# Decoder trunk on one core: every second half unit of up's weights gets its low part from an accumulating transfer, and the front end is written in another order

## The chip, the cores and the metric

The kernel runs on one core of a Trainium2 chip. Its engines run side by side, each through its own list of instructions in order: PE (matrix products), ACT (scalar engine), DVE (vector engine), POOL (GpSimd) and SP (here a queue that issues transfers); ACT and POOL issue transfers too. The metric is the device time of one execution in microseconds (us), as the median of several runs.

## What is computed

Two layers, then a final norm, on 256 tokens of width 1024. Cut to what matters here:

```python
for l in range(2):
    h = rmsnorm(x, g_mix[l])
    proj = h @ w_in[l]                      # 1024 x 8192: q, k, v, gates of two kinds of attention
    ...                                     # retention and stick-breaking attention
    x = x + merged @ w_out[l]
    h = rmsnorm(x, g_mlp[l])
    up = square(relu(h @ w_up[l]))          # w_up: 1024 x 4096
    x = x + up @ w_down[l]                  # w_down: 4096 x 1024
return rmsnorm(x, g_final)
```

All of it is float32. A product is made of three matrix products in a reduced format (fp32r): each operand is split into a high part (the rounded value) and a low part (the value minus the high part), and high x high, high x low and low x high are added.

## The kernel before

**The weights as a stream.** All weight matrices are cut into units of 512 rows x 512 columns (1 MB), listed in the order of use; class WeightStream walks the list. `load` brings a unit into one of 3 raw tiles [128, 4, 512] (SP queue). `_split` works on a half unit [128, 2, 512]: ACT copies it into an fp32r tile `whi` (L73, the high part), DVE subtracts (L78) and writes `wlo` (the low part). There are 4 buffers of `whi` and 4 of `wlo`. `take` hands the next half to the matrix products and first calls `ahead`, which writes the splits up to 3 halves ahead (LOOKAHEAD) and the loads up to 2 units ahead (RAW_AHEAD). So the split of a half starts when PE is through with the half four places earlier, and a unit's load starts when the raw tile three units earlier has been read.

**The products.** `cols512` runs 4 halves into a set of PSUM banks. `half_T` (L281, L283, L285) serves the first projections, `half_W` (L299 with `whi`, L301 with `wlo`) serves k and up, `half_N` (L319 to L321) the rest. For each of the four groups g of the MLP there are 4 units of up (two calls of `cols512`: banks `pa`, then `pb`) and 4 units of down. After each call of up, `evac_up` joins the bank halves (`joined`: ACT copy L308, DVE add L309), takes relu (ACT L721) and square (ACT L722) and splits the result (ACT L180, DVE L181). This evacuation runs beside the next call's halves.

**The front end.** x is brought in four pieces of 256 columns on ACT's queue, the first unit in four pieces and the second in two on SP's queue, then the third unit and the constants `cst`, `tab`, `dec`. PE turns x (`turned`, L204), ACT and DVE apply the gain column and split (`gain_split`, L194 and L195). The gain columns `gcol` of both norms come from one small transposition of `gn` (L174).

**What sets the order.** The kernel is written with tiles; a scheduler puts each engine's instructions in an order at build time and inserts the waits. Some instructions of the front end are pinned to the written order. A wait in a list below such as DMASW1 is for a transfer issued from POOL, DMAHW1 for one issued from SP or ACT, PE_, DVE_ and Activation_ for those engines; the number behind a tile's name tells tiles of one name apart.

Of the kernel before, what the change touches and what calls it, by code (L numbers as in the profile page):

```python
# [10 lines left out]
F32 = mybir.dt.float32  # L11
F32R = mybir.dt.float32r
BF16 = mybir.dt.bfloat16
AF = mybir.ActivationFunctionType
ALU = mybir.AluOpType
PSUM = bass.MemoryType.PSUM

P = 128
# [22 lines left out]
class WeightStream:  # L41

    def __init__(self, nc, pools, units):
        self.nc = nc
        self.raw_pool, self.hi_pool, self.lo_pool = pools
        self.units = units
        self.raw = []
        self.parts = {}  # L50
        self.split = 0
        self.pos = 0
        self.between = self.pin = None

    def load(self, pieces=1, between=lambda j: None):
        u = len(self.raw)
        t = self.raw_pool.tile([P, 4, 512], F32, tag="raw", name=f"raw{u}")
        src = self.units[u].rearrange("(k p) n -> p k n", p=P)
        n = 4 // pieces
        for j in range(pieces):  # L60
            self.nc.sync.dma_start(out=t[:, j * n:(j + 1) * n, :], in_=src[:, j * n:(j + 1) * n, :])
            between(j)
        self.raw.append(t)

    def _split(self, h):
        src = self.raw[h // 2][:, 2 * (h % 2):2 * (h % 2) + 2, :]
        hi = self.hi_pool.tile([P, 2, 512], F32R, tag="hi", name=f"whi{h}")
        lo = self.lo_pool.tile([P, 2, 512], F32R, tag="lo", name=f"wlo{h}")
        for i, sl in enumerate((slice(0, 1), slice(1, 2)) if h < 2 else (slice(0, 2),)):
            if h == 0 and i == 0:  # L70
                self.nc.vector.tensor_copy(out=hi[:, sl], in_=src[:, sl])
            else:
                m = self.nc.scalar.copy(out=hi[:, sl], in_=src[:, sl])  # L73
                if h < 3:
                    self.pin(m)
            if h == 0:
                self.between(i)
            m = self.nc.vector.tensor_tensor(out=lo[:, sl], in0=src[:, sl], in1=hi[:, sl].bitcast(F32),  # L78
                                             op=ALU.subtract)
            if h < 3:  # L80
                self.pin(m)
        self.parts[h] = (hi, lo)
# [16 lines left out]
def kernel(ctx, tc, x, w_in, p_ret, p_sb, w_out, w_up, w_down, g_mix, g_mlp, g_final,  # L99
                      c_sq, c_tab, c_decay, out):  # L100
    nc = tc.nc
    const = ctx.enter_context(tc.tile_pool(name="const", bufs=1))
    big = ctx.enter_context(tc.tile_pool(name="big", bufs=1))
    raw_pool = ctx.enter_context(tc.tile_pool(name="raw", bufs=3))
    hi_pool = ctx.enter_context(tc.tile_pool(name="hi", bufs=4))
    lo_pool = ctx.enter_context(tc.tile_pool(name="lo", bufs=4))
    wk = ctx.enter_context(tc.tile_pool(name="wk", bufs=2))
    small = ctx.enter_context(tc.tile_pool(name="small", bufs=2))
    psA = ctx.enter_context(tc.tile_pool(name="psA", bufs=4, space=PSUM))
    psB = ctx.enter_context(tc.tile_pool(name="psB", bufs=4, space=PSUM))  # L110


    units = []

    def add(w, r0, c0):
        units.append(w[r0:r0 + 512, c0:c0 + 512])

    def add_cols(w, c0, n):
        for c in range(c0, c0 + n, 512):
            add(w, 0, c)  # L120
            add(w, 512, c)

    for l in range(DEPTH):
        for n, wd in (("q_s", 1024), ("k_s", 1024), ("v_s", 1024), ("q_r", 512), ("k_r", 512),
                      ("v_r", 1024), ("g_r", 1024), ("g_a", 1024), ("g_b", 1024)):
            add_cols(w_in[l], OFF[n], wd)
        for c in (0, 512):
            for w in (p_sb[l], p_ret[l]):
                add(w, 0, c)
                add(w, 512, c)  # L130
        add_cols(w_out[l], 0, D)
        for g in range(4):
            add_cols(w_up[l], g * 1024, 1024)
            for c in (0, 512):
                add(w_down[l], g * 1024, c)
                add(w_down[l], g * 1024 + 512, c)


    xs = big.tile([P, 2, D], F32, tag="x", name="x")
    xv = x[0].rearrange("(t p) d -> p t d", p=P)  # L140
    ident = const.tile([P, P], F32, name="ident")
    gn = const.tile([32, P], F32, name="gn")
    ws = WeightStream(nc, (raw_pool, hi_pool, lo_pool), units)
    tc.keep_in_program_order(nc.scalar.preload_act_table_set("natural_log_exp_and_others"))
    nc.scalar.dma_start(out=ident, in_=c_sq[:, 0, :])
    nc.sync.dma_start(out=gn[0:16, :], in_=g_mix.rearrange("l (k p) -> (l k) p", p=P))
    nc.sync.dma_start(out=gn[16:32, :], in_=g_mlp.rearrange("l (k p) -> (l k) p", p=P))
    for j in range(4):
        c = slice(j * 256, (j + 1) * 256)
        nc.scalar.dma_start(out=xs[:, :, c], in_=xv[:, :, c])  # L150
    ws.load(4)
    ws.load(2)
    ws.load()
    cst = const.tile([P, 2, P], F32, name="cst")
    nc.sync.dma_start(out=cst, in_=c_sq[:, 1:3, :])
    tri_f, ones = cst[:, 0, :], cst[:, 1, :]
    tab = const.tile([P, 2, S], F32, name="tab")
    nc.sync.dma_start(out=tab, in_=c_tab)
    dec = const.tile([P, RH + 1, S], F32, name="dec")
    nc.sync.dma_start(out=dec, in_=c_decay)  # L160


    warm = wk.tile([P, 512], F32, tag="t2", name="warm").bitcast(BF16)[:, 0:512]
# [3 lines left out]
    def busy(n):  # L167
        for _ in range(n):
            tc.keep_in_program_order(nc.tensor.matmul(wps, lhsT=warm[:, 0:P], rhs=warm, start=True, stop=True))

    busy(WARM)

    gps = psA.tile([P, 512], F32, tag="a", name="gps")
    nc.tensor.transpose(gps[:, :32], gn, ident[0:32, 0:32])  # L174
    gcol = const.tile([P, 32], F32, name="gcol")
    nc.scalar.copy(out=gcol, in_=gps[:, :32])
    busy(2)

    def split_to(hi, lo, src):
# [37 lines left out]
    def rstd_rows(r):  # L217

        dg = wk.tile([P, 2, S], F32, tag="t1", name="dg")[:, 0, :]
        for t in range(2):  # L220
            nc.vector.tensor_scalar(dg[:, t * P:(t + 1) * P], ident, r[:, t:t + 1], None, ALU.mult)
        bc = psB.tile([P, 512], F32, tag="b", name="bc")
        nc.tensor.matmul(bc[:, :S], lhsT=ones, rhs=dg, start=True, stop=True)
        rb = wk.tile([P, S], F32, tag="rb", name="rb", bufs=1)
        nc.vector.tensor_copy(out=rb, in_=bc[:, :S])
        return rb

    class Norm:


        def __init__(self, gi):
            self.gi = gi
            self.ms = small.tile([P, 4], F32, tag="ms4", name="ms4")
            self.h = paired("h", "h")
# [109 lines left out]
    between = []  # L344
# [13 lines left out]
    def paired(tag, name):  # L358

        return [big.tile([P, 2, 2, S], F32R, tag=f"{tag}{i}", name=name) for i in range(4)]  # L360
# [13 lines left out]
    onesr = const.tile([P, P], F32R, name="onesr")  # L374

    def mix(l, norm):
        h = norm.h
        state = {"n": 0}


        def norm_tick():
            state["n"] += 1
            if l == 0 and state["n"] <= 4:
                tc.keep_in_program_order(norm.square(*divmod(state["n"] - 1, 2)))
            if state["n"] == 4:
                state["rc"] = norm.rstd()
                if l == 0:
                    tc.keep_in_program_order(nc.vector.tensor_copy(out=trir, in_=tri_f))
                    nc.vector.tensor_copy(out=onesr, in_=ones)
            if state["n"] == 5:  # L390
                rc = state["rc"]
                rb = rstd_rows(rc)
                rcs = small.tile([P, 2], F32, tag="rcs", name="rcs")
                nc.vector.tensor_scalar(rcs, rc[:, 0:2], P ** -0.5, None, ALU.mult)
                cr = wk.tile([P, S], F32, tag="cr", name="cr", bufs=1)
                sr = wk.tile([P, S], F32, tag="sr", name="sr", bufs=1)
                nc.vector.tensor_tensor(out=cr, in0=tab[:, 0, :], in1=rb, op=ALU.mult)
                nc.vector.tensor_tensor(out=sr, in0=tab[:, 1, :], in1=rb, op=ALU.mult)
                state.update(rb=rb, rcs=rcs, cr=cr, sr=sr)
            if state["n"] == 6:  # L400
                state["evac"]()

        qs = paired("q", "qs")
        q1 = big.tile([P, SH, P], F32, tag="qb", name="q1")
# [14 lines left out]
        def put_v(hi, lo, src, t):  # L419
            nc.scalar.activation(hi, src, AF.Identity, scale=rc[:, t:t + 1])  # L420
            nc.vector.scalar_tensor_tensor(out=lo, in0=src, scalar=rc[:, t:t + 1], in1=hi.bitcast(F32),
                                           op0=ALU.mult, op1=ALU.subtract)

        banks0 = cols512(half_T, h, norm_tick)
        state["evac"] = lambda: evac_q(0, banks0)
        evac_q(1, cols512(half_T, h, norm_tick))
        rc, rb, rcs = state["rc"], state["rb"], state["rcs"]
        for c in range(2):
# [312 lines left out]
    for l in range(DEPTH):  # L741
        norm = mlp(l, mix(l, norm))
# [46 lines left out]
```

## Time and profile before

| | us |
|---|---|
| median of 3 runs (914.57 to 915.81) | 914.61 |
| the profiled execution's own time | 914.65 |
| its span, first to last instruction | 912.9 |
| PE busy | 903.2 (99%) |
| DVE busy | 609.6 (67%) |
| ACT busy | 523.2 (57%) |
| POOL busy, 18 instructions | 9.6 (1%) |

The busy share is an average over the whole span. Which engine holds the others is read from the waits: who stood idle, until what, and for how long, in the stretch that is spoken of. The chain of work that ended last, followed back from the end, lies on PE for 97% of the span.

### The profile page before, as it was taken

How to read it: one execution, taken by the hardware profiler on the slowest of the kernel's cores; microseconds unless marked ns; L12 is line 12 of the kernel's file. 1: busy time of each engine (PE TensorE's matmuls, PEld its weight loads, DVE VectorE, ACT ScalarE, POOL GpSimd, SP SyncE). 2: the span in 40 equal slices, each digit the busy share in tenths (PEclk: the TensorE clock that was granted, in tenths of full speed). 3: DMA queues.
4: the chain of work that ended last, by engine and by line, in shares of the span. 5: the costliest groups of instructions: out<-in, count | busy, mean ns of one | idle time of the engine just before them, and what ended most of it. 6: DMA issues, size and time to landing. Idle time of an engine off the chain costs nothing.

```text
span 912.9 us, 12229 instructions
## 1 busy us (share of the span) xinstructions
PE 903.2 (99%) x4830; PEld 777.0 (85%) x4830; DVE 609.6 (67%) x798; ACT 523.2 (57%) x733; POOL 9.6 (1%) x18
## 2 busy tenths in 40 slices
PE   8999999999999999999999999999999999999997
PEld 6989988888888888888898898888888888888886
DVE  5765995675666656666666579757656666666665
ACT  6556586554456655555655557665534574646473
POOL 0000000000000000000000000000000000000000
PEclk9999999999999999999999999999999999999999
DMA  9655355446555655555555545545555555555641
GB/s 329 195 190 173 131 185 185 139 141 207 187 185 163 203 192 198 186 185 185 185 185 185 185 147 174 164 161 154 192 185 185 184 186 184 185 190 185 204 160 47
DMA packets 82825, 163.92 MB, mean 180 GB/s; under 512 B 2736, under 2 KB 4048, under 8 KB 82768
## 3 DMA queue, kind: packets, MB, share of 16 engines
q1 hardware_dynamic: 81104, 160.98, 53.9%
q10 hardware_dynamic: 1664, 2.16, 0.8%
q8 instruction: 38, 0.62, 0.3%
q14 instruction: 19, 0.16, 0.0%
HBM read 162.09 MB, written 1.05 MB: 179 GB/s over the span
## 4 chain that ended last, share of the span: by engine, by line
PE 97%; DMA 1%; ACT 0%; SPq 0%; DVE 0%; POOLq 0%; issue 0%; ACTq 0%
PE pa L319 17%; PE pa L321 17%; PE pa L320 17%; PE pb L299 8%; PE pa L299 8%; PE pb L301 4%; PE pa L301 4%; PE pa L281 3%; PE pa L283 3%; PE pa L285 3%; PE pb L319 2%; PE pb L321 2%; PE pb L320 2%; DMA raw<-in_w_in_dram 1%; PE tp L204 1%; PE rop L580 1%
## 5 line engine op out<-in xcount | busy, mean ns | idle before, releaser
L78 DVE TENSOR_TENSOR wlo<-raw,whi 128x1024 fp32r<-128x1024 f32 (+1 forms) x306 | 371.9, 1217 | 242.5 <-ACT whi L73 239.3
L73 ACT CAST whi<-raw 128x1024 fp32r<-128x1024 f32 (+1 forms) x305 | 318.7, 1045 | 318.8 <-PE pa L320 195.2
L299 PE MATMUL pa<-h,whi 128*128 128x512 f32 x320 | 113.3, 398 | 0.0
L299 PE MATMUL pb<-h,whi 128*128 128x512 f32 x320 | 113.1, 397 | 0.0
L319 PE MATMUL pa<-whi,h 128*128 128x512 f32 x256 | 102.1, 399 | 0.0
L321 PE MATMUL pa<-wlo,h 128*128 128x512 f32 x256 | 100.0, 391 | 0.0
L320 PE MATMUL pa<-whi,h 128*128 128x512 f32 x256 | 99.8, 390 | 0.0
L319 PE MATMUL pa<-whi,up 128*128 128x512 f32 x240 | 93.5, 390 | 0.0
L320 PE MATMUL pa<-whi,up 128*128 128x512 f32 x240 | 93.5, 389 | 0.0
L321 PE MATMUL pa<-wlo,up 128*128 128x512 f32 x240 | 93.4, 389 | 0.0
L301 PE MATMUL pb<-h,wlo 128*128 128x256 f32 x320 | 89.8, 281 | 0.0
L301 PE MATMUL pa<-h,wlo 128*128 128x256 f32 x320 | 89.8, 281 | 0.0
L281 PE MATMUL pa<-h,whi 128*128 128x256 f32 x256 | 73.6, 289 | 1.5 <-ACT whi L73 1.5
L299 PEld LDWEIGHTS pa<-h,whi 128*128 128x128 f32 x320 | 60.1, 188 | 14.5
L299 PEld LDWEIGHTS pb<-h,whi 128*128 128x128 f32 x320 | 60.1, 188 | 14.5
L285 PE MATMUL pa<-h,wlo 128*128 128x256 f32 x256 | 72.1, 284 | 0.2 <-DVE wlo L78 0.2
L283 PE MATMUL pa<-h,whi 128*128 128x256 f32 x256 | 72.3, 284 | 0.0
L301 PEld LDWEIGHTS pa<-h,wlo 128*128 128x128 f32 x320 | 60.4, 189 | 0.3
L301 PEld LDWEIGHTS pb<-h,wlo 128*128 128x128 f32 x320 | 60.5, 189 | 0.0
L321 PEld LDWEIGHTS pa<-wlo,h 128*128 128x128 f32 x256 | 48.1, 188 | 10.6
L320 PEld LDWEIGHTS pa<-whi,h 128*128 128x128 f32 x256 | 48.2, 188 | 8.8
L319 PEld LDWEIGHTS pa<-whi,h 128*128 128x128 f32 x256 | 48.1, 188 | 8.8
(173 smaller groups left out, 1415.9 us busy)
## 6 DMA issues: line engine op xcount, KB each, us to landing
raw<-in_w_in_dram SPq DMA_DIRECT2D x62, 1024.0 KB, 5.4
raw<-in_w_up_dram SPq DMA_DIRECT2D x32, 1024.0 KB, 5.3
raw<-in_w_down_dram SPq DMA_DIRECT2D x32, 1024.0 KB, 5.0
raw<-in_p_sb_dram SPq DMA_DIRECT2D x8, 1024.0 KB, 5.1
raw<-in_p_ret_dram SPq DMA_DIRECT2D x8, 1024.0 KB, 5.3
raw<-in_w_out_dram SPq DMA_DIRECT2D x8, 1024.0 KB, 5.0
x<-in_x_dram ACTq DMA_DIRECT2D x4, 256.0 KB, 5.3
raw<-in_w_in_dram SPq DMA_DIRECT2D x4, 256.0 KB, 5.6
```

Of the source, the lines that this page charges most:

```text
L73: m = self.nc.scalar.copy(out=hi[:, sl], in_=src[:, sl])
L78: m = self.nc.vector.tensor_tensor(out=lo[:, sl], in0=src[:, sl], in1=hi[:, sl].bitcast(F32), op=ALU.subtract)
L204: m = nc.tensor.transpose(tp[:, a * S + t * P:a * S + (t + 1) * P], src(t)[:, f:f + P], ident)
L281: nc.tensor.matmul(dst, lhsT=whi[:, kk, cols], rhs=ahi, start=st, stop=False, skip_group_check=True)
L283: nc.tensor.matmul(dst, lhsT=whi[:, kk, cols], rhs=alo, start=False, stop=False, skip_group_check=True)
L285: nc.tensor.matmul(dst, lhsT=wlo[:, kk, cols], rhs=ahi, start=False, stop=sp, skip_group_check=True)
L299: nc.tensor.matmul(banks[o], lhsT=whi[:, kk, cols], rhs=a.rearrange("p a b -> p (a b)"), start=first and kk == 0, stop=False, skip_group_c ...
L301: nc.tensor.matmul(banks[o][:, S:2 * S], lhsT=wlo[:, kk, cols], rhs=a[:, 0, :], start=False, stop=last and kk == 1, skip_group_check=True)
L319: nc.tensor.matmul(banks[t], lhsT=ahi, rhs=whi[:, kk, :], start=st, stop=False)
L320: nc.tensor.matmul(banks[t], lhsT=alo, rhs=whi[:, kk, :], start=False, stop=False)
L321: nc.tensor.matmul(banks[t], lhsT=ahi, rhs=wlo[:, kk, :], start=False, stop=sp)
L580: nc.tensor.matmul(op[:, o:o + S], lhsT=sc[:, i, a:b], rhs=vr[hd][:, t, j, :], start=(n == 0 and a == 0), stop=(n == 2 and t == 1), skip_g ...
```

## The change

For the units of up (32 in all), the second half of each is split in another way: ACT copies the high part as before, ACT then writes minus the high part into `wlo`, and a transfer issued from POOL adds the raw tile to it in place. The first halves, and all other weights, are split as before. In the front end, `gn` becomes two tiles with 16 rows each, the second loaded and turned later (`columns(1)`, in the sixth `norm_tick`); the constants are loaded in the first `norm_tick`; x comes as two pieces of 256 columns on ACT's queue and one of 512 columns on SP's queue behind the first unit; the first unit is cut 1, 1, 2 instead of 1, 1, 1, 1.

```diff
-    def load(self, pieces=1, between=lambda j: None):
+    def load(self, pieces=(4,), between=lambda j: None):
...
-        n = 4 // pieces
-        for j in range(pieces):
-            self.nc.sync.dma_start(out=t[:, j * n:(j + 1) * n, :], in_=src[:, j * n:(j + 1) * n, :])
+        a = 0
+        for j, n in enumerate(pieces):
+            self.nc.sync.dma_start(out=t[:, a:a + n, :], in_=src[:, a:a + n, :])
+            a += n
             between(j)
...
+        if h % 2 and h // 2 in self.by_dma:
+
+            lo = self.lo_pool.tile([P, 2, 512], F32R, tag="lo", name=f"wlo{h}")
+            self.nc.scalar.copy(out=hi, in_=src)
+            self.nc.scalar.mul(lo, hi.bitcast(F32), -1.0)
+            self.nc.gpsimd.dma_start(out=lo.bitcast(F32), in_=src, accum_op=ALU.add)
+            self.parts[h] = (hi, lo)
+            return
...
         for g in range(4):
+            by_dma.update(range(len(units), len(units) + 4))
             add_cols(w_up[l], g * 1024, 1024)
...
-    nc.sync.dma_start(out=gn[0:16, :], in_=g_mix.rearrange("l (k p) -> (l k) p", p=P))
-    nc.sync.dma_start(out=gn[16:32, :], in_=g_mlp.rearrange("l (k p) -> (l k) p", p=P))
-    for j in range(4):
-        c = slice(j * 256, (j + 1) * 256)
-        nc.scalar.dma_start(out=xs[:, :, c], in_=xv[:, :, c])
-    ws.load(4)
-    ws.load(2)
+    nc.sync.dma_start(out=gn[0], in_=g_mix.rearrange("l (k p) -> (l k) p", p=P))
+    load_x(nc.scalar, 0, 2)
+    ws.load((1, 1, 2), lambda j: load_x(nc.scalar, 2, 4) if j == 0 else None)
+    load_x(nc.sync, 4, 8)
+    ws.load((2, 2))
     ws.load()
...
+    def columns(i):
+
+        gps = psA.tile([P, 512], F32, tag="a", name="gps")
+        nc.tensor.transpose(gps[:, :16], gn[i], ident[0:16, 0:16])
+        nc.scalar.copy(out=gcol[:, 16 * i:16 * i + 16], in_=gps[:, :16])
+
+    columns(0)
...
             state["n"] += 1
+            if l == 0 and state["n"] == 1:
+                load_constants()
...
             if state["n"] == 6:
                 state["evac"]()
+                if l == 0:
+                    columns(1)
```

**ACT, group g = 1 of layer 0, the evacuation of the first call of up.** `raw_2940` is the fourth unit of up in this group, `raw_2988` the first of down. Before:

```order
245 L308 COPY wh<-pa 128x256 [waits PE_49] x2
246 L308 COPY wh<-pa 128x256 [waits DVE_49,PE_49]
247 L73 CAST whi_3078<-raw_2940 128x1024 [waits PE_49]
248 L721 ACTIVATE u<-u 128x512 [waits DVE_49]
249 L308 COPY wh<-pa 128x256 [waits PE_49,Activation_49]
250 L722 ACTIVATE u<-u 128x512 [waits Activation_49]
251 L180 CAST up<-u 128x2x256 [waits Activation_49]
252 L721 ACTIVATE u<-u 128x512 [waits DVE_49]
253 L73 CAST whi_3100<-raw_2988 128x1024 [waits DMAHW6_49,PE_49]
```

Now, where the same unit is `raw_2947`, the first of down `raw_2996`, and line 747 is what line 722 was:

```order
251 L329 COPY wh<-pa 128x256 [waits PE_49] x2
252 L329 COPY wh<-pa 128x256 [waits DVE_49,PE_49]
253 L73 CAST whi_3087<-raw_2947 128x1024 [waits PE_49]
254 L746 ACTIVATE u<-u 128x512 [waits DVE_49]
255 L329 COPY wh<-pa 128x256 [waits PE_49,Activation_49]
256 L747 ACTIVATE u<-u 128x512 [waits Activation_49]
257 L74 ACTIVATE wlo_3088<-whi_3087 128x1024 [waits DMASW5_49]
258 L201 CAST up<-u 128x2x256 [waits Activation_49]
259 L746 ACTIVATE u<-u 128x512 [waits DVE_49]
260 L83 CAST whi_3110<-raw_2996 128x1024 [waits DMAHW4_49,PE_49]
```

The negation (row 257) stands not right behind its cast (row 253) but three instructions later, behind the first relu, the last join copy and the first square. In the other three units of a group it stands right behind its cast, except that in group 0 of each layer the second unit's stands behind two squares of the norm.

**SP, the same group: the loads of the third and fourth unit of up and of the first three of down.** Before:

```order
62 L61 DMA raw_2906<-in_w_up_dram 128x4x512 [waits DMAHW1_49,DVE_49]
63 L61 DMA raw_2940<-in_w_up_dram 128x4x512 [waits DMAHW2_49,DVE_49]
64 L61 DMA raw_2988<-in_w_down_dram 128x4x512 [waits DMAHW3_49,DVE_49]
65 L61 DMA raw_3030<-in_w_down_dram 128x4x512 [waits DMAHW4_49,DVE_49]
66 L61 DMA raw_3098<-in_w_down_dram 128x4x512 [waits DMAHW5_49,DVE_49]
```

Now:

```order
63 L62 DMA raw_2912<-in_w_up_dram 128x4x512 [waits DMAHW7_49,DVE_49]
64 L62 DMA raw_2947<-in_w_up_dram 128x4x512 [waits DMASW4_49,DMAHW0_49,DVE_49,Activation_49]
65 L62 DMA raw_2996<-in_w_down_dram 128x4x512 [waits DMASW5_49,DMAHW1_49,DVE_49,Activation_49]
66 L62 DMA raw_3039<-in_w_down_dram 128x4x512 [waits DMASW6_49,DMAHW2_49,DVE_49,Activation_49]
67 L62 DMA raw_3108<-in_w_down_dram 128x4x512 [waits DMASW7_49,DMAHW3_49,DVE_49,Activation_49]
```

Four loads of each group now wait for an accumulating transfer (DMASW), since that transfer is the last reader of the raw tile.

**PE, the front end, where the second unit's first half begins.** `whi_207` belongs to the second unit, `whi_252` to the third. Before:

```order
73 L281 MATMUL pa<-h,whi_207 128x256 [waits Activation_49]
74 L281 MATMUL pa<-h,whi_207 128x256
75 L281 MATMUL pa<-h,whi_252 128x256 [waits Activation_49]
76 L283 MATMUL pa<-h,whi_252 128x256
77 L281 MATMUL pa<-h,whi_252 128x256 [waits PE_49]
78 L283 MATMUL pa<-h,whi_252 128x256
79 L283 MATMUL pa<-h,whi_207 128x256 [waits DVE_49]
80 L285 MATMUL pa<-h,wlo_208 128x256
```

Now (`whi_206` is the second unit, `whi_251` the third; rows 73 to 78 are products with `whi_206` and `wlo_207` as well, row 75 the first that waits for DVE):

```order
79 L306 MATMUL pa<-h,wlo_207 128x256
80 L304 MATMUL pa<-h,whi_206 128x256
81 L306 MATMUL pa<-h,wlo_207 128x256
82 L302 MATMUL pa<-h,whi_206 128x256
83 L304 MATMUL pa<-h,whi_206 128x256
84 L306 MATMUL pa<-h,wlo_207 128x256
85 L225 MATMUL tp<-ident,x 128x128 x4
86 L302 MATMUL pa<-h,whi_206 128x256 [waits Activation_49]
87 L302 MATMUL pa<-h,whi_206 128x256
88 L302 MATMUL pa<-h,whi_251 128x256
```

The first product with the third unit has moved from the third place of this half to behind its first twelve products and a turn of x. Further on, the second turn of `gn` (now L194) stands on PE behind the first twelve products of the seventh half and waits for DVE, which empties the bank that it is given.

## Rows read from the trace of the kernel before

**Rows 1.** Who PE waited for: engine, line, released by, us in total, times, longest.

```profile
PE pa L281 <- ACT whi L73: 1.5, 1, 1.5
```

**Rows 2.** Busy time by stretch: from:to, length; PE, PEld, DVE, ACT, POOL (instructions); clock, DMA share, GB/s.

```profile
14.84:16.84 2.00, 0.51 (x3) 0.30 (x3) 1.43 (x3) 1.10 (x2) 0.00 (x0) 1.00 1.07 410
16.84:20.00 3.16, 3.16 (x27) 3.16 (x28) 3.06 (x4) 2.35 (x5) 0.00 (x0) 1.00 1.02 385
336.11:347.42 11.31, 11.31 (x67) 9.80 (x65) 7.67 (x11) 8.54 (x15) 0.00 (x0) 1.00 0.53 181
```

**Rows 3.** Groups by line on ACT and DVE, both calls of up, 324.82 to 347.42.

```profile
L73 ACT CAST whi<-raw 128x1024 fp32r<-128x1024 f32 x8 | 8.4, 1047 | 8.8 <-PE pa L299 5.4 <-PE pb L299 1.7 <-PE pa L320 1.7
L78 DVE TENSOR_TENSOR wlo<-raw,whi 128x1024 fp32r<-128x1024 f32 x8 | 9.8, 1225 | 8.1 <-ACT whi L73 8.0
```

**Rows 4.** Timeline of ACT there: start, duration, what, idle before and its releaser.

```profile
324.79 1.05 ACT L73 CAST whi<-raw 128x1024 fp32r<-128x1024 f32 x1 [1.67 <-PE pa L320]
...
336.36 1.05 ACT L73 CAST whi<-raw 128x1024 fp32r<-128x1024 f32 x1
337.31 0.64 ACT L721 ACTIVATE u<-u 128x512 f32<-128x512 f32 x1
...
338.09 0.64 ACT L722 ACTIVATE u<-u 128x512 f32<-128x512 f32 x1
338.77 0.62 ACT L180 CAST up<-u 128x512 fp32r<-128x512 f32 x1
...
339.83 1.03 ACT L73 CAST whi<-raw 128x1024 fp32r<-128x1024 f32 x1
```

**Rows 5.** Timeline of PE there: first low products of two halves, and the second call's start.

```profile
333.52 0.28 PE L301 MATMUL pa<-h,wlo 128*128 128x256 f32 x1
...
336.11 0.40 PE L299 MATMUL pb<-h,whi 128*128 128x512 f32 x1
...
344.83 0.28 PE L301 MATMUL pb<-h,wlo 128*128 128x256 f32 x1
```

**Rows 6.** Transfers of the page: issues, KB each, median us from issue to landing.

```profile
raw<-in_w_up_dram SPq DMA_DIRECT2D x32, 1024.0 KB, 5.3
raw<-in_w_down_dram SPq DMA_DIRECT2D x32, 1024.0 KB, 5.0
```

**Rows 7.** The same for transfers issued in the first 24 us.

```profile
raw<-in_w_in_dram SPq DMA_DIRECT2D x4, 1024.0 KB, 8.7
...
gn<-in_g_mix_dram SPq DMA_DIRECT2D x1, 8.0 KB, 1.8
```

**Rows 8.** Timeline of SP: one load.

```profile
327.12 0.37 SPq L61 DMA_DIRECT2D raw<-in_w_down_dram  x1
```

**Rows 9.** What all transfers moved, in 40 slices of 326 to 333 us.

```profile
GB/s 281 176 105 94 0 0 0 0 0 0 0 0 129 129 94 117 117 211 398 398 339 410 410 421 410 386 398 421 421 433 316 24 12 0 0 0 0 0 0 0
```

**Rows 10.** Timeline of the front end, PE.

```profile
6.56 0.58 PE L281 MATMUL pa<-h,whi 128*128 128x256 f32 x1
...
16.84 0.39 PE L281 MATMUL pa<-h,whi 128*128 128x256 f32 x1 [1.50 <-ACT whi L73]
...
35.11 0.40 PE L299 MATMUL pb<-h,whi 128*128 128x512 f32 x1
```

**Rows 11.** Timeline of the front end, ACT.

```profile
12.43 2.00 ACT L73 CAST whi<-raw 128x1024 fp32r<-128x1024 f32 x2
14.31 0.47 ACT L194 ACTIVATE h<-tp,gcol 128x256 fp32r<-128x256 f32 x1
15.74 1.04 ACT L73 CAST whi<-raw 128x1024 fp32r<-128x1024 f32 x1 [0.95 <-DMA raw<-in_w_in_dram]
```

**Rows 12.** Timeline of the front end, DVE.

```profile
13.50 2.36 DVE L78 TENSOR_TENSOR wlo<-raw,whi 128x1024 fp32r<-128x1024 f32 x2 [1.06 <-ACT whi L73]
15.77 0.48 DVE L195 SCALAR_TENSOR_TENSOR h<-tp,gcol,h 128x256 fp32r<-128x256 f32 x1
...
29.19 1.28 DVE L414 TENSOR_TENSOR u<-pa,rb 128x512 f32<-128x512 f32 x2
```

More of the change, by code (lines that the diff above doesn't have):

```diff
@@ L41, with __init__ @@
 class WeightStream:
-    def __init__(self, nc, pools, units):
+    def __init__(self, nc, pools, units, by_dma):
         self.nc = nc
         self.raw_pool, self.hi_pool, self.lo_pool = pools
+        self.by_dma = by_dma
         self.units = units
@@ L113 @@
     units = []
+    by_dma = set()
     def add(w, r0, c0):
@@ L141, with load_x, load_constants @@
     ident = const.tile([P, P], F32, name="ident")
-    gn = const.tile([32, P], F32, name="gn")
-    ws = WeightStream(nc, (raw_pool, hi_pool, lo_pool), units)
+    gn = [const.tile([16, P], F32, name="gn") for _ in range(2)]
+    ws = WeightStream(nc, (raw_pool, hi_pool, lo_pool), units, by_dma)
     tc.keep_in_program_order(nc.scalar.preload_act_table_set("natural_log_exp_and_others"))
+    def load_x(queue, a, b):
+        queue.dma_start(out=xs[:, :, a * P:b * P], in_=xv[:, :, a * P:b * P])
     nc.scalar.dma_start(out=ident, in_=c_sq[:, 0, :])
-    nc.sync.dma_start(out=gn[0:16, :], in_=g_mix.rearrange("l (k p) -> (l k) p", p=P))
-    nc.sync.dma_start(out=gn[16:32, :], in_=g_mlp.rearrange("l (k p) -> (l k) p", p=P))
-    for j in range(4):
-        c = slice(j * 256, (j + 1) * 256)
-        nc.scalar.dma_start(out=xs[:, :, c], in_=xv[:, :, c])
-    ws.load(4)
-    ws.load(2)
+    nc.sync.dma_start(out=gn[0], in_=g_mix.rearrange("l (k p) -> (l k) p", p=P))
[3 more added lines that the diff above has]
+    ws.load((2, 2))
     ws.load()
     cst = const.tile([P, 2, P], F32, name="cst")
-    nc.sync.dma_start(out=cst, in_=c_sq[:, 1:3, :])
     tri_f, ones = cst[:, 0, :], cst[:, 1, :]
     tab = const.tile([P, 2, S], F32, name="tab")
-    nc.sync.dma_start(out=tab, in_=c_tab)
     dec = const.tile([P, RH + 1, S], F32, name="dec")
-    nc.sync.dma_start(out=dec, in_=c_decay)
+    def load_constants():
+        nc.sync.dma_start(out=gn[1], in_=g_mlp.rearrange("l (k p) -> (l k) p", p=P))
+        nc.sync.dma_start(out=cst, in_=c_sq[:, 1:3, :])
+        nc.sync.dma_start(out=tab, in_=c_tab)
+        nc.sync.dma_start(out=dec, in_=c_decay)
     warm = wk.tile([P, 512], F32, tag="t2", name="warm").bitcast(BF16)[:, 0:512]
@@ L171 @@
     busy(WARM)
-    gps = psA.tile([P, 512], F32, tag="a", name="gps")
-    nc.tensor.transpose(gps[:, :32], gn, ident[0:32, 0:32])
     gcol = const.tile([P, 32], F32, name="gcol")
-    nc.scalar.copy(out=gcol, in_=gps[:, :32])
+    def columns(i):
[3 more added lines that the diff above has]
+    columns(0)
     busy(2)
@@ L388, in norm_tick @@
                     tc.keep_in_program_order(nc.vector.tensor_copy(out=trir, in_=tri_f))
-                    nc.vector.tensor_copy(out=onesr, in_=ones)
+                    tc.keep_in_program_order(nc.vector.tensor_copy(out=onesr, in_=ones))
             if state["n"] == 5:
```

## The prediction

> **What bounds the kernel now.** I read the waits of PE first. In the table of the profile PE is busy for 99% of the span, and the list of who PE waited for has one entry of note: 1.5 us, once, in the front end, for a high part that ACT had still to cast [rows 1]. So nothing but PE's own work and its first microseconds set the time. The stretch that the change touches is up: in one of its calls PE is busy for 11.31 of 11.31 us, DVE for 7.67, ACT for 8.54, and the transfers take 0.53 of the DMA engines [rows 2]. There PE is given each half in time. What has to be read is by how much, since the change makes one half in two later. From the second call's start (336.11) to its fourth half's first low product (344.83) three halves pass, 2.83 us each, and 0.24 us [rows 5]. A split may begin when PE is through with the half four places back, so it has three halves and 0.24 us, 8.7 us, before PE stands still for it.
>
> **What is taken from DVE: worth nothing.** 32 subtractions of 1225 ns go [rows 3], 39 us. In that list DVE itself stood idle before them for 8.0 us, waiting for ACT's casts [rows 3]; PE waits for none of them [rows 1]. Gain 0; no cover is needed.
>
> **What is given to ACT: worth nothing in busy time.** 32 negations of the form of the cast, 1047 ns each [rows 3], 33.5 us. In the busier call (336.11 to 347.42) ACT would be busy for 8.54 + 2 x 1.05 = 10.64 of 11.31 us [rows 2]: it still fits, with 0.67 us to spare. Queued behind the negation of the fourth unit are a split of up, a relu and the first cast of down, which would start about 1 us after 339.83 [rows 4]. That cast belongs to the half behind 344.83, which begins near 347.4; 340.9 and 1.05 for the cast and 1.23 for the subtraction make 343.2. Cost 0.
>
> **What is given to the transfers: the term that decides.** The low part is ready when the cast, the negation and the accumulating transfer are through, one after the other. Two kinds of halves are to be told apart.
>
> The loose kind, 24 of 32: cast at 324.79 [rows 4]; ACT starts the next instruction 0.95 us later (336.36 to 337.31 in the same list), the negation runs from 325.74 to 326.79, POOL issues near 326.85; PE wants the half's first low product at 333.52 [rows 5]. The transfer may take 6.67 us from issue to landing. (The two in group 0 that stand behind the norm's squares start later, but the turn of h delays PE there as well; I count them as loose.)
>
> The tight kind, 8 of 32, the fourth unit of each group: the cast is at 336.36, but the new order puts the negation behind the square at 338.09, where the split at 338.77 stood [rows 4]. So it runs from 338.7 to 339.75, POOL issues near 339.8, PE wants it at 344.83 [rows 5]: 5.03 us.
>
> How long the transfer takes, no row shows; the trace has no accumulating transfer and none issued from POOL. Bounds: it writes 512 KB, and halfway between the 8 KB transfer with 1.8 us [rows 7] and the 1 MB load with 5.0 [rows 6] lies 3.4 us, an estimate for a plain copy of that size. From above, loads of 1 MB that had others before them took 8.7 us [rows 7]. I take 5.0 us, the 1 MB load of down [rows 6], since the sum has to read two operands of 512 KB, the same number of bytes. At 5.0 the loose kind has 1.7 us to spare and the tight kind nothing: 0 us of waiting, by a hair. Ends: 0 (at 3.4) and the 46 us that are worked out below (at 8.7).
>
> The Trainium skill bears on that choice. "Collectives: The Full Stack", section "The bandwidth ceiling: the fold count and why AG ≠ RS ≠ AR", states that an adding transfer emits two reads for a piece and so runs at half a copy's rate. "DMA: Bandwidth & Descriptors", section "Anatomy of one DMA — SWDGE (gpsimd) path", fits a transfer from POOL with 2.0 us and the bytes at 436 GB/s: for 1 MB that gives an estimate of 4.4 us, inside both windows, so the sum by it is the same. No row here shows either.
>
> **What waits behind the transfers.** Each group's fourth load of up and first three of down now wait for an accumulating transfer. Before, the load at 327.12 [rows 8] followed the subtraction of the half cast at 324.79; now it follows a landing at 326.85 + 5.0 = 331.9 and lands 5.0 later, at 336.9. Its first cast is at 339.83 [rows 4]. Cost 0, with 2.9 us of cover. On POOL little is queued: one power for a norm, which no one needs before the group's end.
>
> **The front end: about 0.25 us gained.** PE's one wait is that of 16.84 [rows 10]. In the old order the third product of the second unit's first half needs the third unit, whose cast begins at 15.74, as the load lands, and ends at 16.78 [rows 11]; behind it stand products whose last operand DVE has ready at 15.77 + 0.48 = 16.25 [rows 12]. The new order puts those first. The third unit's bytes are the same and so is their place behind the others, so I keep its landing; the operand of 16.25 hangs on two subtractions on DVE (13.50 to 15.86) and two casts on ACT (12.43 to 14.43) [rows 11, 12], which stay. PE goes on at 16.3 in place of 16.84: -0.55. Against it stands the second turn of the gain columns: it waits on PE for DVE to empty the first banks, which ended at 29.19 + 1.28 = 30.47 [rows 12]. The place on PE is 12 + 24 products ahead of 35.11 [rows 10], at 0.12 us each (3.16 us for 27) [rows 2]: 30.8, and 30.25 with the gain. Wait 0.2, the turn 0.1. Net -0.25. The bounds: at most all of PE's idle time there, 35.11 - 6.56 = 28.55 [rows 10] less 192 products and 14 turns and sums at 0.12 (24.7), so -3.8; at worst that turn of the gain columns loses 0.7 more than the order gains, +0.7, since the norm's row on which DVE's emptying rests is also made later in the new order.
>
> **Sum.** 0 + 0 + 0 - 0.25 against the profiled execution's 914.65 us, which is 0.04 from the median: **914.4 us**.
>
> **Rivals.** First, slower, *the tight halves wait*. The transfer takes 6.2 us: 5.0, about 0.5 for building its list on POOL (an estimate: 9.6 us of POOL for 18 instructions in the table), and about 0.7 for sharing. Rows show that a load has the engines to itself when it moves: from 329 to 331.4 it takes some 400 GB/s [rows 9], 2 us behind its issue at 327.12. In the new order a load is issued whenever an accumulate lands, some 5.7 us apart, and so moves while the next one does. "DMA: Bandwidth & Descriptors", section "Issuing engines are not separate DMA queues", in the Trainium skill says that transfers of all issuers share the same engines. By this rival each of 8 tight halves waits 6.2 - 5.03 = 1.2 us: 9.4 us, 923.8. It decides from 5.3 us on (8 x 0.25 = 2 us). For it: the margin is zero at my own value. Against it: every price that I add has no row, and 3.4 is as near as 6.2.
>
> Second, slower, *all halves wait*: at 8.7 us, the first and third transfer of a group wait 2.0 us (8.7 - 6.67), the second not, as its window holds the first's wait, and the fourth 8.7 - 5.03 - 2.0 = 1.7. That is 5.7 in a group, 46 in all: 960. It decides from 6.7 us on. For it: sharing; against it: DMA is only half busy [rows 2].
>
> Third, faster, *the front end gets back half of its idle time*: about -2 of the 3.8 us, 912.4, without waits in up. For it: x's and the first unit's pieces are sent in the order of use. Against it: DVE's chain to 16.25 does not move by my reading.
>
> **How the numbers follow.** 0.2% is 1.8 us, about what a measurement tells from no change. Forecast 914.4 with 46% (its own range 912.9 to 916.2: same); tight halves wait 28%, 916.5 to 928; all wait 14%, above that; front end faster 12%, 911 to 912.8. That gives faster 0.12, same 0.46, slower 0.42. The range 912.4 to 928 leaves out the far case and half of the faster one.
>
> **What would show it.** Right: no wait of PE for a transfer into the low part; landings within 5 us of POOL's issue; PE goes on near 16.3 in the front end; the loads of down land 3 us before their casts. Wrong: a wait of PE at the fourth half of the second call in each group (first rival), at the second halves of all units (second rival); the 35.11 us row at 33 (third).

## The result, and the profile after

The changed kernel takes 939.12 us (median of 4 runs, 937.64 to 942.33), the kernel before beside it 914.59 (914.48 to 915.81). The ratio is 1.0272, interval 1.0256 to 1.0288: slower by 24.5 us. The forecast was 914.4, and 939.1 lies outside the range. The profiled execution took 937.64 us, its span 935.7, which is 22.8 more than before.

I read the waits of PE first, as before [rows 1]. The list of after (engine and line, released by, us in total, times, longest):

```profile
PE pa L322 <- DMA wlo<-raw: 9.1, 7, 2.0
PE pb L322 <- DMA wlo<-raw: 6.6, 5, 2.6
PE wps L185 <- DVE half L393: 1.2, 1, 1.2
PE pa L304 <- DVE h L216: 1.0, 1, 1.0
PE tp L225 <- DMA x<-in_x_dram: 0.8, 1, 0.8
```

The third row is at PE's first products; it stands with 1.2 us in the list of before too. The first two rows are new, and both are waits for an accumulating transfer. Bank `pa` belongs to the first call of up in a group and `pb` to the second. Each wait ends as a transfer lands, and the landings say which: the seven of `pa` are at the *second* unit of a group (9.1 us), which I had counted as loose, and the five of `pb` at the *fourth* (6.6 us), the tight one.

The page's transfers (issues, KB, median us to landing), and the queue of the new ones (packets, MB, share of 16 engines):

```profile
q1 hardware_dynamic: 81360, 161.51, 52.1%
q0 software_dynamic: 4608, 16.78, 9.6%
...
raw<-in_w_up_dram SPq DMA_DIRECT2D x32, 1024.0 KB, 5.5
raw<-in_w_down_dram SPq DMA_DIRECT2D x32, 1024.0 KB, 6.4
wlo<-raw POOLq DMA_DIRECT2D x32, 512.0 KB, 5.1
```

The median of the new transfers is 5.1, where I had taken 5.0, and the loads of down went from 5.0 [rows 6] to 6.4. But the median hides the case that decides. Here is group 2 of layer 0: the three transfers of its first three units on POOL, the one load between them on SP, and PE at the second unit (start, duration, what, idle before and its releaser):

```profile
373.43 0.86 POOL L75 DMA_DIRECT2D wlo<-raw  x1 [25.31 <-ACT wlo L74]
378.87 0.86 POOL L75 DMA_DIRECT2D wlo<-raw  x1 [4.58 <-ACT wlo L74]
384.62 0.86 POOL L75 DMA_DIRECT2D wlo<-raw  x1 [4.89 <-ACT wlo L74]
```

```profile
378.08 0.37 SPq L62 DMA_DIRECT2D raw<-in_w_up_dram  x1
```

```profile
384.92 0.39 PE L320 MATMUL pa<-h,whi 128*128 128x512 f32 x1
387.29 0.39 PE L322 MATMUL pa<-h,wlo 128*128 128x256 f32 x1 [1.97 <-DMA wlo<-raw]
```

From issue to landing, all 32 transfers, then the one issued at 373.43 and the one issued at 378.87, each in an answer for its own stretch:

```profile
DMA to landing us min/median/max: 4.5/5.1/8.4
```

```profile
DMA to landing us min/median/max: 4.5/4.5/4.5
```

```profile
DMA to landing us min/median/max: 8.4/8.4/8.4
```

The first lands at 373.43 + 4.51 = 377.94. It was the last reader of its raw tile, so SP issues the load that had waited for that tile 0.14 us later, at 378.08. The second transfer is issued at 378.87; it lands at 387.24, and PE, which has stood idle at its first low product since 385.3, goes on at 387.29. The queues show that the second transfer's bytes come behind the load's. Here is what each queue moved from 378.0 to 382.4, and then from 382.4 to 387.3 (packets, MB, share of 16 engines; q1 is the loads' queue, q0 that of POOL's transfers, and the second stretch holds the third transfer's first bytes too):

```profile
q1 hardware_dynamic: 404, 0.83, 66.5%
```

```profile
q0 software_dynamic: 205, 0.77, 80.5%
q1 hardware_dynamic: 124, 0.22, 13.5%
```

Up to 382.4, 3.5 us behind its issue, the second transfer moves nothing, while 0.83 MB of the load pass. The first transfer, with no load near it, had begun to move 1.4 us behind its issue.

In the eight groups the first transfer took 4.5 to 4.7 us, the second 6.1 to 8.4 (above 7.7 in six), the third 4.8 to 5.9, the fourth 4.5 to 7.8. The second is issued 0.8 us behind a load in these six groups, and 1.7 and 1.8 us behind it in the two where it took 6.3 and 6.1. The third is issued ahead of the next load.

**The clock.** The second part of the loss is not waiting. Busy time by stretch (from:to, length; PE, PEld, DVE, ACT, POOL; granted clock, DMA share, GB/s), of after:

```profile
300.86:303.48 2.62, 0.00 (x1) 0.00 (x0) 1.60 (x2) 0.74 (x1) 0.00 (x0) 0.87 0.18 34
303.60:310.40 6.80, 6.80 (x22) 5.72 (x23) 2.22 (x4) 3.15 (x7) 0.00 (x0) 0.56 0.87 296
310.40:317.20 6.80, 6.80 (x32) 5.61 (x31) 4.40 (x6) 4.73 (x8) 0.00 (x0) 1.00 0.53 167
384.90:388.90 4.00, 2.03 (x10) 1.53 (x9) 1.65 (x2) 1.42 (x2) 0.58 (x1) 0.90 0.88 159
388.90:392.30 3.40, 3.40 (x15) 2.92 (x14) 0.85 (x2) 1.54 (x3) 0.00 (x0) 0.61 0.99 356
```

PE waits 2.6 us before 303.5 and 2.0 before 387.3, and with each wait the granted clock falls towards the lower of its two levels, 1.2 GHz: 0.56 for 6.8 us and 0.61 for 3.4 us. It shows as fewer products: 22 in 6.80 us, then 32 in the next 6.80. The kernel before, in the first of these two stretches:

```profile
303.60:310.40 6.80, 6.80 (x32) 5.60 (x31) 4.81 (x7) 6.30 (x10) 0.00 (x0) 1.00 0.63 209
```

One minus the granted clock, times the length, gives 0.3, 3.0, 0.4 and 1.3 us for the four stretches below 1.00. The first is the wait itself, in which a lower clock costs nothing; the others add up to 4.7 us. Of the four executions the two longest, 940.40 and 942.33 us, have a mean granted clock of 0.992 and 0.990, where the profiled one has 0.994.

**The account.** The two waiting rows are 15.7 us; taken as gaps between products beyond the usual step (1.70 us between starts in place of 0.24, where the list says 1.31), the same 12 places come to 17.6. The clock costs 4.7. The front end gives back 0.46: the first product of the second call of projections starts at 34.65, where it was 35.11 [rows 10]. 17.6 + 4.7 - 0.5 = 21.8 of the 22.8 us; for the last 1.0 I have no place.

### The profile page after: what moved, and what is told of

It is laid out like the page before. It is cut to its first block, busy times and chain, and to the rows that moved or that the text cites. A ratio compares the mean times of both kernels' runs of the same rounds, so it can differ in the third digit from the quotient of the medians.

```text
span 935.7 us, 12355 instructions
## 1 busy us (share of the span) xinstructions
PE 910.3 (97%) x4831; PEld 780.6 (83%) x4831; DVE 572.5 (61%) x766; ACT 556.8 (59%) x766; POOL 37.5 (4%) x50
## 3 DMA queue, kind: packets, MB, share of 16 engines
q1 hardware_dynamic: 81360, 161.51, 52.1%
HBM read 162.09 MB, written 1.05 MB: 174 GB/s over the span
## 4 chain that ended last, share of the span: by engine, by line
PE 71%; DMA 13%; issue 12%; ACT 2%; DVE 1%; POOLq 0%; POOL 0%
PE pa L340 12%; PE pa L341 12%; PE pa L342 12%; DMA wlo<-raw 10%; PE pb L320 4%; PE pa L320 4%; PE pa L304 3%; PE pa L302 3%; PE pa L306 3%; DMA raw<-in_w_up_dram 3%; PE pb L322 2%; PE pa L322 2%; PE pb L340 2%; PE pb L341 2%; PE pb L342 2%
## 5 line engine op out<-in xcount | busy, mean ns | idle before, releaser
L88 DVE TENSOR_TENSOR wlo<-raw,whi 128x1024 fp32r<-128x1024 f32 (+1 forms) x274 | 332.8, 1216 | 264.6 <-ACT whi L83 257.9
L83 ACT CAST whi<-raw 128x1024 fp32r<-128x1024 f32 (+1 forms) x273 | 284.9, 1044 | 256.0 <-PE pa L341 164.2
L322 PE MATMUL pa<-h,wlo 128*128 128x256 f32 x320 | 91.4, 286 | 9.1 <-DMA wlo<-raw 9.1
L306 PE MATMUL pa<-h,wlo 128*128 128x256 f32 x256 | 72.6, 285 | 0.0
```

The source lines that it names most:

```text
L306: nc.tensor.matmul(dst, lhsT=wlo[:, kk, cols], rhs=ahi, start=False, stop=sp, skip_group_check=True)
L322: nc.tensor.matmul(banks[o][:, S:2 * S], lhsT=wlo[:, kk, cols], rhs=a[:, 0, :], start=False, stop=last and kk == 1, skip_group_check=True)
```

## The experiments

Two theories were put against each other. *Sharing*: an accumulating transfer takes some 4.5 us when it has the DMA engines to itself, and waits arise only where it meets the load that the transfer before it released. *Rivals*: the transfer is slow in itself (A), or comes too late since the negation does (B).

### The two halves of the change apart

The front end alone (label front_only), the line that marks the units of up taken out of the kernel after:

```diff
-            by_dma.update(range(len(units), len(units) + 4))
```

> The changed kernel without the accumulating transfers: all low parts on DVE again, the front end as changed. Theory (sharing: the loss lies in up alone, the front end is right): 0.4 to 0.5 us faster than before, about 914.1, with PE's row at 35.11 us of before at 34.65; no wait of PE for a transfer. Rival (the new front end carries part of the loss, through the loads that it moves): over 916.

Measured: 914.26 us against 914.58, ratio 0.9993 (0.9984 to 1.0002); span 912.5.

```profile
PE pa L303 <- DVE h L215: 0.9, 1, 0.9
PE tp L224 <- DMA x<-in_x_dram: 0.8, 1, 0.8
```

The 1.5 us wait for a cast [rows 1] has gone, and two shorter ones have come: for x's first piece, and for a part of h that DVE makes. The 0.3 us cannot be told from no change. PE's row of 35.11 [rows 10] stands at 34.87 here, not at the 34.65 that I expected.

The transfers alone (label dma_only), the kernel before with the new split only:

```diff
...
+        if h % 2 and h // 2 in self.by_dma:
+            self.nc.scalar.copy(out=hi, in_=src)
+            self.nc.scalar.mul(lo, hi.bitcast(F32), -1.0)
+            self.nc.gpsimd.dma_start(out=lo.bitcast(F32), in_=src, accum_op=ALU.add)
+            self.parts[h] = (hi, lo)
+            return
...
+            by_dma.update(range(len(units), len(units) + 4))
```

> The kernel before with the accumulating transfers alone, the old front end. Theory: the whole loss, 0.5 us more than the changed kernel: 938 to 941, waits of PE in up of 15 to 18 us. Rival (the loss comes from both parts meeting): clearly under 930.

Measured: 938.11 us, ratio 1.0255 (1.024 to 1.027).

```profile
PE pa L310 <- DMA wlo<-raw: 9.8, 6, 2.0
PE pb L310 <- DMA wlo<-raw: 6.5, 5, 2.6
PE pa L290 <- ACT whi L80: 1.7, 1, 1.7
```

The whole loss is here, with the same waits; the third row is the front end's old one.

### Without the loads

The loads of the MLP's units taken away (label no_mlp_loads): of the 32 units of each layer's MLP the first three are loaded, and the others use those raw tiles again. So the values of up and down are not those of the reference; every cast, negation, accumulating transfer and product stays, and so does the time at which each could begin.

```diff
+        if u in self.reuse:
+            self.raw.append(self.raw[u - 3])
+            return
...
+        reuse.update(range(len(units) + 3, len(units) + 32))
...
```

> The changed kernel, but of each layer's 32 MLP units only the first three are loaded; the others use those three raw tiles again (so their weights are wrong), and the splits, the negations, the accumulating transfers and their order stay. Theory (the second transfer of each group is slow because a load that the first one's landing releases moves at the same time): all 32 transfers land in 4.5 to 5.1 us, PE waits under 1 us in all of up, 914 to 916. Rival A (an accumulating transfer is slow in itself, or by what ACT and DVE do at that place): the second of each group still takes 6 to 8 us and PE waits 10 us or more, over 925. Rival B (the late negation of the fourth unit, the tight halves): PE waits about 1 us in each of 8 fourth halves, 920 to 924.

Measured: 916.07 us, ratio 1.0012 (1.0003 to 1.0022). The one wait of PE for a transfer, and the transfers' times:

```profile
PE pb L328 <- DMA wlo<-raw: 0.5, 1, 0.5
...
DMA to landing us min/median/max: 4.5/4.5/6.0
```

With no load beside them nearly all transfers take 4.5 us, negations stand where they stood, and 15.7 us of waiting shrink to 0.5. Sharing holds; A and B fall as causes of the bulk. Three of the 32 took 5.3 to 6.0 us with no load beside them, more than I expected; why stays open.

### Which units

One transfer in each call of up: the first unit's (label one_per_call), or the second's (label second_per_call).

```diff
-            by_dma.update(range(len(units), len(units) + 4))
+            by_dma.update((len(units), len(units) + 2))
```

> The changed kernel with only the first unit of each call of up by accumulating transfer (16 in place of 32). Theory (sharing): the load that such a landing releases has moved before the next accumulating transfer is issued, 11 us after the last; all 16 land in 4.5 to 5 us, no wait of PE, 914 to 915. Rival (each such transfer costs PE about the same): half the loss, 926.

```diff
-            by_dma.update(range(len(units), len(units) + 4))
+            by_dma.update((len(units) + 1, len(units) + 3))
```

> The same with only the second unit of each call (16), among them the fourth unit of each group, whose negation stands behind the evacuation. Theory (sharing): no load is released beside them, so they land in 4.5 to 5 us; the second unit has 1.5 us to spare, the fourth some 0.3; PE waits under 2 us in all, 914 to 916. Rival (these halves are the slow ones by their place on ACT): 6 to 8 us each and the loss of the changed kernel, over 930.

Measured: one_per_call 914.68 us, ratio 0.9997 (0.9988 to 1.0006), no wait of PE for a transfer; second_per_call 916.01, ratio 1.0012 (1.0003 to 1.0021). Their transfers' times, one_per_call's first, then second_per_call's wait and times:

```profile
DMA to landing us min/median/max: 4.5/4.6/5.2
```

```profile
PE pb L322 <- DMA wlo<-raw: 1.1, 2, 0.8
...
DMA to landing us min/median/max: 4.5/4.6/5.7
```

The loads are all there again, and one landing still releases one load; but the next unit has no transfer for that load to meet. Neither set of 16 costs more than about 1.3 us, and the 32 together cost 24: it is the neighbour that costs. Half of the transfers is also half of their work for the engines, and these two runs alone do not tell the one from the other. The places in the changed kernel do: at the same amount of work the first and third transfer of a group take 4.5 to 5.9 us, and the second, issued 0.8 us behind a load, 7.7 to 8.4. Second_per_call holds all 8 tight halves, with the negation behind the evacuation, and they wait 1.1 us in all.

### The other half of each unit

The first half of each unit by transfer in place of the second (label first_halves).

```diff
-        if h % 2 and h // 2 in self.by_dma:
+        if h % 2 == 0 and h // 2 in self.by_dma:
```

> The changed kernel with the first half of each of the 32 units by accumulating transfer in place of the second; no negation then stands behind an evacuation. Theory (sharing): the landing still releases the raw tile, later than the subtraction of the second half, so the second transfer of a group still meets a load: 7 to 8 us there, PE waits over 1 us in each group, 924 to 938. Rival (the late negation is the cause): no waits, 914 to 916.

Measured in one run: 941.64 us, span 939.7, above the range that I expected.

```profile
PE pa L322 <- DMA wlo<-raw: 15.4, 8, 2.9
PE pb L322 <- DMA wlo<-raw: 1.5, 3, 0.8
...
DMA to landing us min/median/max: 4.5/5.3/9.2
```

The order around the evacuation is another one, the fourth unit waits little, and the second unit's transfer takes 7.7 to 9.2 us in all eight groups and makes PE wait in each. In group 1 the fourth unit's negation stands one join copy behind its cast, no longer behind relu and square. B has little left here, and the time is no better.

### A plain copy of the same size

The accumulation left out (label plain_copy): the transfer writes the raw tile over the negated high part, so the low parts of these halves are not low parts. Sizes, order and waits stay.

```diff
-            self.nc.gpsimd.dma_start(out=lo.bitcast(F32), in_=src, accum_op=ALU.add)
+            self.nc.gpsimd.dma_start(out=lo.bitcast(F32), in_=src)
```

> The changed kernel, but the transfer copies the raw tile over the low part in place of adding it (so the low part is wrong): one operand read, not two. Theory (what counts are the bytes read that share the engines): alone 3.3 to 4.0 us, beside a load 5 to 6.5 us, so PE waits under 3 us in all, 914 to 918. Rival (the issue from POOL and the landing set the length, not the bytes): lengths as in the changed kernel within 0.3 us, and 935 to 940.

Measured in one run: 924.43 us, span 922.5, a miss: the expected gain came only in part.

```profile
q0 software_dynamic: 4608, 16.78, 4.5%
...
PE pb L322 <- DMA wlo<-raw: 7.2, 8, 2.0
...
DMA to landing us min/median/max: 2.8/4.5/7.6
```

The first transfer of a group takes 2.8 to 3.0 us, and the second 3.5 to 5.3; no second unit waits now (`pa` is gone from the list). But the third and fourth take up to 7.6, and PE waits at three third and five fourth units. A shorter transfer alone does not mend it.

The queue's share prices the engines' work. 9.6% of 935.7 us is 89.8 us of all 16 engines for 32 accumulating transfers, 2.8 us each; 4.5% of 922.5 is 1.3 for a copy; and a load of 1 MB is 52.1% of 935.7 over 154 units (161.51 MB at 1.05 MB), 3.2 us. An accumulating transfer of 512 KB occupies the engines nearly as long as a load. Alone it takes 4.5; with a whole load ahead of its bytes, 4.5 + 3.2 = 7.7, where six of the eight second transfers lie or a little above. For the copy the same sum is 2.84 + 3.2 = 6.0; its second transfers stay below that, some of its third and fourth above it. The trace shows what sets them apart: the second ones are issued 2.4 to 3.5 us behind a load, the seven third and fourth ones that took 5.9 us or more only 0.3 to 1.2 us behind one. A first copy that lands earlier lets the load go earlier, and so further ahead of the second copy, but the third and fourth still follow close behind a load.

"Collectives: The Full Stack", section "The bandwidth ceiling: the fold count and why AG ≠ RS ≠ AR", of the Trainium skill says of the reducing step of a collective that it reads two sources for a piece and so runs at half the rate of a copying one. The engines' time here agrees, 2.8 against 1.3 us; from issue to landing it is 4.5 against 2.84, of which 1.7 and 1.5 us are not the engines' time.

### The front end once more

The front end alone with x's first piece on SP and `gn` on ACT (label front2), to see whether the new wait for x can be had back.

```diff
...
-    nc.sync.dma_start(out=gn[0], in_=g_mix.rearrange("l (k p) -> (l k) p", p=P))
-    load_x(nc.scalar, 0, 2)
+    load_x(nc.sync, 0, 2)
+    nc.scalar.dma_start(out=gn[0], in_=g_mix.rearrange("l (k p) -> (l k) p", p=P))
```

> The front end alone (no accumulating transfers), with x's first piece issued first on SP's queue and the gain rows on ACT's. PE waited 0.8 us for that piece in the new front end, and later 0.9 us for an operand from DVE at 16.3 us. Theory (the operand at 16.3 sets the end of the front end): the first wait goes, the second grows, 914.0 to 914.3, no change against the front end alone. Rival (x's first piece sets it): 0.5 to 0.8 us faster than the front end alone, 913.5.

Measured: 914.39 us, ratio 0.9995 (0.9986 to 1.0003).

```profile
PE gps L193 <- DMA gn<-in_g_mix_dram: 1.4, 1, 1.4
PE pa L303 <- DVE h L215: 1.0, 1, 1.0
```

The wait for x has gone and one for `gn` has come; the 1.0 us wait for DVE's operand stays, and with it the end of this stretch. No gain.

Not tried: a fourth raw tile, or more buffers of the high and low parts, since they do not fit into the memory that the kernel has left. None of the kernels beats both by more than its interval.

## Why the prediction was wrong

**What bounds the kernel, and DVE: right.** PE stayed the bound, and taking 32 subtractions from DVE gave nothing: one_per_call takes 16 of them and stands at 0.9997.

**ACT: right in busy time, 0.4 us short in the chain.** I gave each loose half 6.67 us, with 0.95 us from the cast's start to the negation's. The trace has the cast, the negation and POOL's issue so:

```profile
325.26 1.05 ACT L73 CAST whi<-raw 128x1024 fp32r<-128x1024 f32 x1 [1.67 <-PE pa L341]
326.35 1.06 ACT L74 ACTIVATE wlo<-whi 128x1024 fp32r<-128x1024 f32 x1
...
327.71 0.86 POOL L75 DMA_DIRECT2D wlo<-raw  x1 [31.16 <-ACT wlo L74]
```

The 0.95 was between two instructions that don't depend on each other; the negation reads what the cast writes and starts 1.09 behind the cast's start, and POOL issues 0.3 behind the negation's end, where I had 0.06. From cast to issue it is 2.45 us in place of 2.06, so the loose window was about 6.3 us. The tight one, where the negation stands behind the square anyway, lost only POOL's part and was about 4.8.

**The transfer: the step that failed.** I sized it 5.0 us from the load of down, as one number for all places. Alone it takes 4.5, below my value, and 4.5 fits the loose window of 6.3 and, with 0.3 to spare, the tight one of 4.8: second_per_call with its 1.1 us in all is that forecast come true. "DMA: Bandwidth & Descriptors", section "Anatomy of one DMA — SWDGE (gpsimd) path", of the Trainium skill gave an estimate of 4.4 for it, and the trace agrees with its 4.5. What was missing is the transfer's price to the engines beside a load, 6.1 to 8.4 us at the second unit. The number was in reach: the up stretch used 0.53 of the engines [rows 2], 3.0 us of each unit's 5.66 (two halves of 2.83), and my own reading that the transfer moves 1 MB adds about what a load takes. Measured, it is 3.2 + 2.8 = 6.0 us of engine time for a unit that lasts 5.66. Over the four transfers of group 1 the share in the trace of after is 0.83:

```profile
327.71:347.30 19.59, 18.28 (x101) 15.55 (x100) 6.76 (x9) 12.15 (x16) 2.62 (x4) 1.00 0.83 212
```

So the engines still had idle time there, and what decides is that a transfer comes close behind a load. I read "DMA is only half busy" as room, and did not add what the change puts into it.

**What waits behind the transfers: no wait of PE for a load, but wrong as a cost of 0 and in its cover.** No wait of PE for a cast in up is in the list. The 2.9 us of cover that I gave the first load of down were not there: in group 1 it lands at 346.75 and its cast begins at 347.90, and in four of the eight groups the cast begins as the load lands. In group 0 of layer 0, where it lands at 296.78:

```profile
296.86 1.05 ACT L83 CAST whi<-raw 128x1024 fp32r<-128x1024 f32 x1 [0.43 <-DMA raw<-in_w_down_dram]
```

Gating a load by a landing moves it from beside the split to just ahead of the *next* transfer, 0.14 us after one landed and 0.8 before the next is issued. I wrote down this very clash in the first rival, and charged 0.7 us for it, to the tight halves alone. Measured, it is 1.6 to 3.9 us at the second unit. "DMA: Bandwidth & Descriptors", section "Issuing engines are not separate DMA queues", of the Trainium skill, cited there, says that the transfers of all issuers run on the same engines and interleave. The trace agrees with the first; of interleaving it shows little, since up to 382.4 only the load's bytes moved.

**The rivals.** The first named the mechanism and had the wrong place: the tight halves waited 6.6 us (9.4 foretold), the loose ones 9.1 (0 foretold). The second had the length (8.7), but for every transfer alike; only second ones, and some fourth, came near it. The measured time lies in the second's bracket, above 928, to which I gave 14%, by the first's mechanism and a clock that neither had. The third fell.

**The front end: held.** PE went on at 16.33 (16.3 foretold) for a wait of 0.96 us on DVE:

```profile
16.33 0.39 PE L304 MATMUL pa<-h,whi 128*128 128x256 f32 x1 [0.96 <-DVE h L216]
...
34.65 0.40 PE L320 MATMUL pb<-h,whi 128*128 128x512 f32 x1
```

Net -0.46 in the trace of after and -0.24 in that of front_only (-0.25 foretold); the -0.3 of front_only's time is inside its interval. The wait of 0.2 that I gave the second turn of the gain columns is not in the list. The wait for x (0.8) was not foreseen; PE would have waited for DVE's operand all the same, as front2 shows.

**The clock: not in the sum.** I priced waits at their length. Two of twelve brought a lower clock with them, 4.7 us in all, some 30% on top of 15.7.

## What to carry to other kernels

A new transfer has two prices: the time from its issue to its landing alone, and the time for which it occupies the DMA engines; add the second to the stretch's share before calling the engines free. Where the transfer is the last reader of a buffer, its landing releases the next load, and that load goes just ahead of the next transfer of the series; so price it behind a load, place by place, by how long before the transfer that load is issued. And where PE has no slack, a wait of some 2 us can cost more than its length.

## What was not expected of the hardware

- Adding in the transfer: 4.5 us for 512 KB alone where a copy takes 2.84, and 0.86 us of POOL for each issue where a copy takes 0.53.
- The clock at a wait is not settled by the wait's length alone. In after it fell with waits of 2.6 and 2.0 us, and not with one of 1.8; in dma_only with one of 2.6, and not with one of 2.0. In first_halves it fell in up with waits of 1.75, 2.24, 2.38 and 2.51 us, and not with 1.80 and 2.94. What else decides stays open.
- Order in the DMA engines: a transfer issued 0.8 us behind a load moved nothing until most of the load had passed (0.83 of 1.05 MB).
